# Projection weights in two parts, the first attention unit's loads ahead of the windowed ones, and the last tile's multiplies on VectorE

## The chip, the cores and the metric

The kernel runs on one core of a Trainium2 chip. The metric is the device time of one execution in microseconds (us). The engines named below are TensorE (PE), VectorE (DVE), ScalarE (ACT), GpSimd (POOL) and SyncE (SP), which here only issues DMAs.

## The reference

One layer of a bidirectional encoder on 2048 tokens of width 1024, in float32:

```python
h = rms_norm(x, ln1_g)
z = h @ w_in         # [q_A 512 | k_A 128 | v_A 128 | c_q 384 | c_kv 256 | k_rope 32]
o_A = window_gqa(...)        # |i-j| <= 128, 8 heads, 2 kv heads, table of biases, sink logit
o_B = latent_attention(...)  # q from c_q @ w_qb, k and v from c_kv @ w_kvb, one rotary key
                             # for all heads, 8 heads, dense over 2048 keys
x = x + concat(rms_norm(o_A), rms_norm(o_B)) @ w_o
x = x + expert_choice_ffn(rms_norm(x))   # 16 experts, each takes 256 tokens
```

Queries and keys are RMS-normalised per head; the rotary parts are turned by position.

## The kernel before, in words

The program has three regions. **Region 1** takes the sixteen 128-token tiles one by one: RMSNorm, transposes, the projection with w_in, and from its result everything that attention needs. The result is stored to HBM in transposed form: `kT`, `qT`, `kR` and `v2` for latent attention (stage s3, lines L808 to L830, and stage s2, L720 to L806), `qA`, `kA`, `vA_d` for windowed attention (stage sa, L680 to L718). **Region 2** computes the windowed attention of 16 query tiles (`bounded(t)`, L998 to L1047) interleaved with 32 units of latent attention (8 heads by 4 chunks of 512 queries, `head(h, qc)`, L1107 to L1174). A window tile is two or three pairs of score matmuls (L1016), a table add on DVE (L1021), an exponential on ACT (L1024), adds into `acw` on POOL (L1026, L1028), value matmuls (L1033) and the row sums (L1055, which take `ones` from an operand that depends on the sink row `es`, L1065 and L1066). A latent unit is four groups of rotary matmuls (L1126), score matmuls (L1135), exponentials (L1140), value matmuls (L1150) and adds into `acc` on DVE (L1143, L1145). **Region 3** is w_o, the router and the experts.

Every matmul operand is split into a high part (ACT, L419) and a low part (DVE, L421), and a projection is three products. The w_in weights, split in this way, fill one SBUF tile `WB` of 128 x 23040 words. When the projections of the last tile have run, the same tile is carved anew (class `Views`, L298 to L313) into the bias table, the windowed keys, queries and values, the first unit's queries `qq0`, and the latent keys and values. What is loaded there waits for a marker operation `MK` behind the last projection matmul. For the last tile the transposed results also lie in `WB`; for the others they lie in the two buffers of `th`.

The order of the work on each engine is made by a list planner before the program is built (`Plan.schedule`, L147 to L241). An operation has a cost, a priority (its stage's number plus an offset per stage and engine, `OFF1` for region 1, `OFF2` for region 2) and a list of what it needs; the planner lets each engine take the ready operation of least priority. So a changed cost, need or offset can reorder instructions in the whole region. SP is an engine like the others: a DMA whose data isn't there holds back the DMAs behind it in its queue. In the kernel, SP's DMAs also go round eight completion semaphores, so that each waits until the one eight places ahead has landed.

`PRE_K` is the number of key tiles of the first latent unit that are loaded before the branch that ends region 1 (L1727); the rest of its keys is loaded behind the branch.

Of the kernel before, what the change touches and what calls it, by code (L numbers as in the profile page):

```python
# [21 lines left out]
P = 128  # L22
# [22 lines left out]
PRE_K, PRE_PR = 8, 155  # L45
OFF1 = {'s1S': -41.3, 's2V': 236.2, 's2P': -164.3, 's3V': -16.5, 'saS': 38.9, 's3S': 457.6, 'saV': -26.6, 's3P': -240.0, 'saG': -311.4, 's2G': -35.2, 's1P': -67.4, 's1A': -127.1, 's2A': 17.7, 's2S': -117.5, 's3A': -334.6, 'saA': 265.7, 's1V': -588.0, 'saP': 172.4}
OFF2 = {'bfP': -89.2, 'aG': -6.5, 'awV': -1.5, 'bfS': -57.7, 'bfV': 89.2, 'asP': -33.4, 'awP': -84.8, 'bfA': -1.0, 'bfG': -6.1, 'bvP': 29.3, 'awS': -37.9, 'avP': 28.4, 'afS': 47.0, 'blS': -30.5, 'bV': 10.7, 'pfS': 58.5}
# [211 lines left out]
def build(tc, nc, a, out, dbg=None, upto=9, path="both"):  # L259
# [38 lines left out]
    class Views:  # L298


        def __init__(self):
            carve = carver()
            self.tab = f(carve(8, 384))
            kk = carve(4 * 6 * P)
            self.KK = {n: kk[:, :4 * n * P].rearrange("p (c s) -> p c s", c=4) for n in (4, 6)}
            self.qq0 = carve(3, 512)
            self.va = f(carve(4, 2, 64))
            self.qs = [carve(8, P), None]
            self.kr = carve(4, P)
            v0, k0 = f(carve(NT, VD)), carve(2, SEQ)  # L310
            self.free = WB[:, carve.used[0]:]
            v1, k1 = f(carve(NT, VD)), carve(2, SEQ)
            self.vts, self.kk = [v0, v1], [k0, k1]  # L313
# [36 lines left out]
        def fetch_qq(self, h, qc, qq):  # L350
            src = qT[:, h * HD:h * HD + HD, qc * 512:qc * 512 + 512]

            def go():
# [5 lines left out]
                for j in range(4):  # L359
                    sync.dma_start(q[RD * j:RD * j + RD, 2], src[1, NO:HD])  # L360
# [27 lines left out]
    class Ops(Plan):  # L388
# [25 lines left out]
        def load(self, nbytes, fn, r, w, need=(), pr=None):  # L414
            return self.op("S", 0.5, fn, r, w, need, pr, nbytes)
# [24 lines left out]
    def region1():  # L440
        with ExitStack() as st:
# [16 lines left out]
            WH, WL = (pl.fixed(carve(ND, CW + AW)) for _ in range(2))  # L458
# [39 lines left out]
            load_w(WH, WL, a["w_in"][0][:, AW:], lambda: g1, ND, CW, -30)  # L498
# [4 lines left out]
            load_w(WH, WL, a["w_in"][0][:, :AW], lambda: g1, ND, AW, -8, CW)  # L503
# [23 lines left out]
            MK = pl.fixed(None)  # L527
# [85 lines left out]
            def stage1(t):  # L613
# [26 lines left out]
                def project(c0, n, need):  # L640
                    z = [u_(), u_()]
                    for k in range(ND):
                        xh, xl = xT[k // 4]

                        def mms(k=k, xh=xh, xl=xl):
                            for lh, rh, first, last in ((xh, WH, k == 0, False), (xh, WL, False, False),
                                                        (xl, WH, False, k == ND - 1)):
                                for i in range(2):
                                    pe.matmul(z[i]()[:, :n], lh()[:, k % 4, :], rh()[:, k, c0 + i * n:c0 + (i + 1) * n],  # L649
                                              start=first, stop=last)  # L650

                        pl.mm(6 * n / 2400, mms, [xh, xl, (WH, (k, c0)), (WL, (k, c0))], z, need=need)
# [3 lines left out]
                z = project(0, 336, [zc])  # L656
# [16 lines left out]
            def th_(t, shape, i):  # L673
# [4 lines left out]
                return pl.fixed(V2.free[:shape[0], 1024 * i:1024 * i + 2 * n * P].rearrange("p (a b c) -> p a b c", a=2, b=n))  # L678

            def stage_a(t):  # L680
                s1, project = S[t][3:]
                rows = slice(t * P, (t + 1) * P)
                za = z3([P, 12, 64])
                z = project(CW, 384, [za])
                if t == NT - 1:
                    pl.op("P", 0.0, lambda: None, [], [WH, WL, MK], pr=-99)
# [6 lines left out]
                pl.G(640, lambda: pool.tensor_mul(sq(), za()[:, :10], za()[:, :10]), [(za, 0), (za, 1)], [sq])  # L693
# [10 lines left out]
                pl.G(512, lambda: pool.tensor_mul(za()[:, :8], za()[:, :8], bh(r1()[:, :8], 64)), [r1, (za, 0), (za, 1)],  # L704
                     [(za, 3)])
                for dst, h0, n in ((kA, 8, 1), (qA, 0, 4)):
# [7 lines left out]
                    pl.mm(n * TR, trs, [(za, 2 if h0 else 3)] + ([MK] if t == NT - 1 else []), [tr], need=[th])  # L714
# [5 lines left out]
            def stage2(t):  # L720
                zc, v3, r3 = S[t][:3]
# [86 lines left out]
            def stage3(t):  # L808
# [4 lines left out]
                for i, (src, dst, c0, n) in enumerate(((ks, kT, 0, 4), (qf, qT, 0, 4), (qf, qT, 4, 2))):  # L813
# [7 lines left out]
                    pl.mm(n * TR, trs, [src] + ([MK] if t == NT - 1 else []), [tr], need=[th])  # L821
# [941 lines left out]
```

## Time and profile before

| | |
|---|---|
| time, median of 3 runs | 2586.59 us (2585.72 to 2591.03) |
| profiled execution | 2585.55 us |
| its span (first to last instruction) | 2583.8 us |
| PE busy | 2461.3 us, 95% of the span |
| DVE, ACT, POOL busy | 63%, 46%, 13% |
| region 1 | until about 439.5 us, projections until 428.6 us |
| region 2 | from about 440 us to 1180 us |

A row of a timeline gives an instruction's start, its duration, the engine, the line, the output and the inputs. In square brackets stands how long the engine had been idle before it, and what ended the idle time. SPq rows are the issues of DMAs; the transfer itself ends later. The granted clock is the speed that TensorE was given, 1.00 standing for 2.4 GHz and 0.50 for 1.2 GHz.

### The profile page before, as it was taken

Reading aid. Unit: us, or ns where it says so; the run is one execution under the profiler, and the core shown is the slowest. Engines: PE = TensorE matmul, PEld = TensorE weight load, DVE = VectorE, ACT = ScalarE, POOL = GpSimd, SP = SyncE. Lnnn points to the kernel's source line nnn. Section 1 sums busy time; section 2 is a strip of 40 time slices with the busy share of each in tenths; the row PEclk is TensorE's granted clock in tenths of the full one; section 3 lists DMA queues with packets and bytes.
Section 4 is the critical chain, followed back from the end, with each engine's and each line's share of the span. In section 5 each row is a group of like instructions: output and inputs, shape, how many; then the busy total and the mean of one; then the engine's idle time right before and its main releaser. Section 6 shows DMA issues by size and latency. Waiting matters only on the chain.

```text
span 2583.8 us, 38603 instructions
## 1 busy us (share of the span) xinstructions
PE 2461.3 (95%) x14922; PEld 1962.1 (76%) x14922; DVE 1636.5 (63%) x3024; ACT 1195.1 (46%) x1729; POOL 335.6 (13%) x268
## 2 busy tenths in 40 slices
PE   6999997899999999998997599999999999999998
PEld 5999996344444444446786599999999999999997
DVE  6666665586777767668767765555555555555553
ACT  5444543444444444444444344454554445454442
POOL 2233232121111210000000000000000000000000
PEclk9999998899999999999999699999999999999999
DMA  6433435942442333116543266666666666766662
GB/s 195 131 117 115 120 98 157 212 113 67 104 107 74 90 87 81 55 44 217 174 162 132 74 203 211 204 206 217 215 215 202 223 215 210 226 200 219 220 189 81
DMA packets 348544, 399.40 MB, mean 155 GB/s; under 512 B 43152, under 2 KB 291856, under 8 KB 348224
## 3 DMA queue, kind: packets, MB, share of 16 engines
q1 hardware_dynamic: 339136, 363.03, 44.9%
q0 software_dynamic: 9216, 33.82, 5.4%
q8 instruction: 119, 1.95, 0.3%
q14 instruction: 73, 0.60, 0.1%
HBM read 317.47 MB, written 81.41 MB: 154 GB/s over the span
## 4 chain that ended last, share of the span: by engine, by line
PE 87%; DVE 5%; issue 3%; DMA 2%; ACT 1%; POOL 1%; SPq 1%; POOLq 0%; DVEq 0%; ACTq 0%
PE y L1675 14%; PE u L649 10%; PE gu L1645 9%; PE gu L1646 9%; PE gu L1647 9%; PE sb L1135 9%; PE pv L1150 7%; PE y L1370 6%; PE u L743 3%; PE sb L1126 2%; PE sb L1055 1%; PE tr L1621 1%; PE sb L1016 1%; DVE acc L1145 1%; PE pv L1033 1%
## 5 line engine op out<-in xcount | busy, mean ns | idle before, releaser
L421 DVE TENSOR_TENSOR wlo<-raw,whi 128x2048 fp32r<-128x2048 f32 x192 | 440.0, 2292 | 364.4 <-ACT whi L419 364.4
L1645 PE MATMUL gu<-xh,whi 128*128 128x256 f32 x2048 | 580.9, 284 | 0.0
L1646 PE MATMUL gu<-xl,whi 128*128 128x256 f32 x2048 | 575.1, 281 | 0.0
L1647 PE MATMUL gu<-xh,wlo 128*128 128x256 f32 x2048 | 574.8, 281 | 0.0
L419 ACT ACTIVATE whi<-raw 128x2048 fp32r<-128x2048 f32 x192 | 368.2, 1917 | 276.9 <-PE gu L1646 150.9
L1140 ACT ACTIVATE pp<-sb 128x1024 f32<-128x1024 f32 x256 | 252.6, 1025 | 303.6 <-PE sb L1135 262.3
L1645 PEld LDWEIGHTS gu<-xh,whi 128*128 128x128 f32 x2048 | 385.9, 188 | 0.6
L1646 PEld LDWEIGHTS gu<-xl,whi 128*128 128x128 f32 x2048 | 385.8, 188 | 0.7
L1647 PEld LDWEIGHTS gu<-xh,wlo 128*128 128x128 f32 x2048 | 385.8, 188 | 0.0
L1145 DVE TENSOR_TENSOR acc<-acc,pp 128x1024 f32<-128x1024 f32 x192 | 248.9, 1297 | 125.0 <-ACT pp L1140 115.2
L1675 PE MATMUL y<-whi,aa 128*128 128x512 f32 x1024 | 278.5, 391 | 0.0
L1150 PE MATMUL pv<-pp,WB 128*64 128x512 f32 x1024 | 252.5, 606 | 0.0
L1675 PEld LDWEIGHTS y<-whi,aa 128*128 128x128 f32 x1024 | 191.3, 188 | 40.4
L649 PE MATMUL u<-WB,xh 128*128 128x384 f32 (+1 forms) x1024 | 219.9, 336 | 2.2 <-ACT WB L419 1.4
L649 PEld LDWEIGHTS u<-WB,xh 128*128 128x128 f32 x1024 | 172.3, 190 | 3.4 <-ACT WB L419 1.8
L1370 PE MATMUL y<-whi,aa 128*128 128x512 f32 x512 | 149.0, 403 | 10.9 <-ACT aa L419 8.7
L1675 PE MATMUL y<-wlo,aa 128*128 128x512 f32 x512 | 158.6, 391 | 0.0
L1150 PEld LDWEIGHTS pv<-pp,WB 128*64 128x64 f32 x1024 | 64.1, 136 | 122.6 <-issue 92.3
L1686 POOL DMA_INDIRECT out_dram<-ot,idx x32 | 51.0, 1594 | 792.8 <-ACT ot L1683 702.0
L1135 PE MATMUL sb<-WB 128*128 128x512 f32 x512 | 142.2, 417 | 0.0
L1135 PE MATMUL sb<-qq,WB 128*128 128x512 f32 x512 | 140.0, 416 | 0.0
L649 PE MATMUL u<-WB,xl 128*128 128x336 f32 (+1 forms) x512 | 126.9, 329 | 0.0
(274 smaller groups left out, 3442.8 us busy)
## 6 DMA issues: line engine op xcount, KB each, us to landing
raw<-w_gate SPq DMA_DIRECT2D x64, 1024.0 KB, 5.1
raw<-w_up SPq DMA_DIRECT2D x64, 1024.0 KB, 5.3
raw<-w_down SPq DMA_DIRECT2D x64, 1024.0 KB, 5.1
xt<-x SPq DMA_DIRECT2D x32, 512.0 KB, 4.1
WB<-kT SPq DMA_DIRECT2D x48, 256.0 KB, 4.6
oT_d<-fo SPq DMA_DIRECT2D x64, 128.0 KB, 2.4
ot<-oT_d SPq DMA_DIRECT2D x16, 512.0 KB, 4.2
out_dram<-xt SPq DMA_DIRECT2D x16, 512.0 KB, 2.7
```

The costliest lines, as they stand in the source:

```text
L419: self.A(n, lambda: act.activation(hi(), src(), AF.Copy, scale=sc()), r + list(rs), [w_hi], need, pr, sb)
L421: self.V(n, lambda: dve.tensor_sub(lo(), src(), f(hi())), r + [w_hi], [w_lo], need, pr)
L649: pe.matmul(z[i]()[:, :n], lh()[:, k % 4, :], rh()[:, k, c0 + i * n:c0 + (i + 1) * n], start=first, stop=last)
L1135: pe.matmul(s()[:, j], kk.t[:, c, ksl], qq()[:, c], start=False, stop=c == 1)
L1140: pl.A(1024, lambda s=s, p=p: act.activation(p(), s(), AF.Exp), [s], [p])
L1145: pl.V(1024, lambda p=p: dve.tensor_add(acc(), acc(), p()), [p], [acc])
L1150: pe.matmul(pv()[64 * j:64 * j + 64], vt()[:, 2 * n + j], p()[:, j], start=n == 0, stop=n == 7)
L1370: pe.matmul(pw[i](), o4(l)[:, ks], r_()[:, c:c + 512], start=first, stop=last_)
L1645: pe.matmul(o, c3(hi, ND)[:, k, fs], xh()[:, k], start=k == 0, stop=False)
L1646: pe.matmul(o, c3(hi, ND)[:, k, fs], xl()[:, k], start=False, stop=False)
L1647: pe.matmul(o, c3(lo, ND)[:, k, fs], xh()[:, k], start=False, stop=k == ND - 1)
L1675: pe.matmul(y[i][j](), l()[:, ts], r_()[:, o:o + 512], start=first, stop=last_)
```

## The change

**Weights in two parts.** The weights of w_in are kept as `W1` (the columns of c_q, c_kv and k_rope, the first 10752 words of a row of `WB`) and `WA` (the columns of the windowed heads). `Views` puts `qq0`, the latent keys and values `k0` and `v0`, the rotary key `kr` and the windowed values `va` over `W1`, and the table, windowed keys and queries over `WA`. Two markers take the place of one: `MK1` behind the last matmul with `W1`, `MK2` behind the last with `WA`.

**Loads and priorities.** The first latent unit's loads need `MK1` and the stores of the key tiles they read; they have priority 140 to 142. Twelve key tiles are loaded instead of eight. The windowed keys and queries and the table need `MK2` and have priority 900 and 901, which lies behind the stores of the last tiles. A unit's queries are fetched by five DMAs instead of eight (the last four become one that reads its source four times).

**Last tile.** The multiplies of 640 and 512 columns in stage sa run on DVE for tile 15.

**Region 2.** The windowed tiles' priorities are moved (`step` 26 in place of 27, and `LATE` 14), and an operation without an instruction on an engine "D" of the planner stands for the table's arrival, 8 us into the region's plan. The offsets are other numbers: in `OFF1` s2P goes from -164.3 to -242.7, s3V from -16.5 to 12.0, saV from -26.6 to -2.9; in `OFF2` bfS, awP, bfA, bvP change, and pfV and bA are added.

```diff
-PRE_K, PRE_PR = 8, 155
+PRE_K, PRE_PR = 12, 140
...
+            self.qq0 = carve(3, 512)
+            v0, k0 = f(carve(NT, VD)), carve(2, SEQ)
+            self.kr = carve(4, P)
+            free1 = carve(2560)
+            self.va = f(carve(4, 2, 64))
+            carve(2 * ND * CW - carve.used[0])
             self.tab = f(carve(8, 384))
...
-                for j in range(4):
-                    sync.dma_start(q[RD * j:RD * j + RD, 2], src[1, NO:HD])
+                sync.dma_start(q[:, 2], src[1, NO:HD][None].to_broadcast([4, RD, 512]))
...
-            WH, WL = (pl.fixed(carve(ND, CW + AW)) for _ in range(2))
+            W1 = [pl.fixed(carve(ND, CW)) for _ in range(2)]
+            WA = [pl.fixed(carve(ND, AW)) for _ in range(2)]
...
-                z = project(0, 336, [zc])
+                z = project(W1, 336, [zc])
+                if t == NT - 1:
+                    pl.op("P", 0.0, lambda: None, [], W1 + [MK1], pr=-99)
...
             def stage_a(t):
+                G_, en = (pl.V, dve) if t == NT - 1 else (pl.G, pool)
...
-                    pl.op("P", 0.0, lambda: None, [], [WH, WL, MK], pr=-99)
+                    pl.op("P", 0.0, lambda: None, [], WA + [MK2], pr=-99)
...
-                pl.G(640, lambda: pool.tensor_mul(sq(), za()[:, :10], za()[:, :10]), [(za, 0), (za, 1)], [sq])
+                G_(640, lambda: en.tensor_mul(sq(), za()[:, :10], za()[:, :10]), [(za, 0), (za, 1)], [sq])
...
-            pl.load(1600000, load_tab, [GD, MK], [], pr=PRE_PR + 1)
+            first = sum((KT[t] for t in range(4)), [MK1])
+            most = sum((KT[t] for t in range(PRE_K)), [MK1])
+            K0 = pl.fixed(None)
+            pl.load(P * 6144, V2.fetch_qq(0, 0, lambda: V2.qq0), first, [(K0, 0)], pr=PRE_PR, n=5)
+            pl.load(P * 512 * PRE_K // 4, V2.fetch_kr(0, PRE_K // 4), most, [(K0, 1)], pr=PRE_PR, n=4)
+            pl.load(P * 8 * PRE_K * P, V2.fetch_k(0, 0, PRE_K * P), most, [(K0, 2)], pr=PRE_PR + 1, n=4)
+            pl.load(PRE_K * P * 256, V2.fetch_v(0, 0, PRE_K), most, [(K0, 3)], pr=PRE_PR + 2)
...
+                pl.load(P * 512, V2.fetch_va(t), QA[t] + [MK1], [], pr=PRE_PR + 2)
...
+                    pl.load(64 * 2048, fn, QA[t] + [MK2], [], pr=900)
+            for fn in V2.fetch_q(0):
+                pl.load(64 * 4096, fn, QA[0] + [MK2], [], pr=900)
+            pl.load(1600000, load_tab, [GD, MK2], [], pr=901)
...
+                pl.op("D", 8.0, lambda: None, [], [TAB], pr=-1000, nbytes=1)
...
-            step = 27 if mix else 10
+            step, LATE = (26, 14) if mix else (10, 0)
...
-                base = step * (t + 1)
+                base = step * (t + 1) + LATE
```

SP before, from the last stores of tile 14's windowed heads to the first DMA behind the branch (L322 and L317 load windowed keys and queries, L872 the table, L355 to L364 the first latent unit; `th` and `WB` on the right of an arrow are stores):

```order
L717 DMA kA<-th_5275 128x2x128
L322 DMA WB<-kA 64x4x128 x2
...
L872 DMA WB<-g_d 128x8x384
L317 DMA WB<-qA 64x8x128 x2
L355 DMA WB<-qT 96x512
...
L335 DMA WB<-kT 64x1024
...
L364 DMA WB<-v_63 128x8x64
L717 DMA qA<-th_5352 128x8x128
L824 DMA kT<-WB 128x4x128 x2
L700 DMA vA_d<-va_5416 128x128
...
L717 DMA qA<-WB 128x8x128
L1727 COMPARE_AND_BRANCH
```

The table and the loads stand ahead of the stores of the last tile. SP after the change, from the same kind of store on (L357 to L365 load the first latent unit, L324 and L319 windowed keys and queries, L885 the table):

```order
L725 DMA kA<-th_4983 128x2x128
L357 DMA WB<-qT 96x512
...
L337 DMA WB<-kT 64x1536
...
L365 DMA WB<-v_63 128x12x64
...
L725 DMA qA<-th_5095 128x8x128
L833 DMA kT<-th_5081 128x4x128 x2
...
L324 DMA WB<-kA 64x4x128 x2
...
L725 DMA kA<-th_5399 128x2x128
...
L885 DMA WB<-g_d 128x8x384
L725 DMA qA<-th_5418 128x8x128
...
L1742 COMPARE_AND_BRANCH
...
L337 DMA WB<-kT 64x512
```

The first unit's loads now stand ahead of the remaining stores of tiles 13 and 14, the windowed loads between the stores, and the table ahead of the last three stores, where `qA<-th_5418` is that of tile 14's queries.

PE before at the branch, from the last transposes of region 1 on (L1016 window scores, L1126 rotary, L1135 latent scores, L1033 and L1150 values):

```order
L712 MATMUL tr_5430<-cm,z_1_5126 128x128
L712 MATMUL tr_5433<-cm,z_1_5126 128x128 x4
L1726 TENSOR_LOAD flag_t
L1727 COMPARE_AND_BRANCH
L1016 MATMUL sb_5496<-WB 128x512 x4
L1016 MATMUL sb_5507<-WB 128x512 x4
L1126 MATMUL sb_5537<-WB 128x512 x2
...
L1135 MATMUL sb_5537<-WB 128x512 x4
...
L1033 MATMUL pv_5498<-pp_5497,WB 64x512 x2
L1150 MATMUL pv_5541<-pp_5539,WB 64x512 x2
```

PE after the change at the same place (L1141 rotary, L1150 latent scores, L1031 window scores, L1165 and L1048 values):

```order
L720 MATMUL tr_5417<-cm,z_0_4820 128x128 x4
L720 MATMUL tr_5425<-cm,z_4_5155 128x128 x4
L720 MATMUL tr_5436<-cm,z_4_5155 128x128
L1741 TENSOR_LOAD flag_t
L1742 COMPARE_AND_BRANCH
L1141 MATMUL sb_5493<-WB 128x512 x2
...
L1150 MATMUL sb_5493<-WB 128x512 x4
...
L1031 MATMUL sb_5515<-WB 128x512 x4
...
L1165 MATMUL pv_5497<-pp_5495,WB 64x512 x2
...
L1048 MATMUL pv_5517<-pp_5516,WB 64x512 x2
```

The latent unit's rotary and score matmuls have gone ahead of the window scores, and of the last transposes those of tile 15's windowed heads (`z_4_5155`) now come last.

POOL before, from the last tile's key multiply to the branch (`z_1_5126` is the last tile's windowed projection, `k_2` its latent keys):

```order
L788 TENSOR_TENSOR k_2_5284<-k_2_5284,r_1_5309 128x512
L693 TENSOR_TENSOR z_0_5346<-z_1_5126 128x640
L789 TENSOR_TENSOR k_2_5284<-k_2_5284,gkn 128x512
L791 TENSOR_TENSOR z_4_5237<-z_4_5237,r_1_5309 128x8x32
L792 TENSOR_TENSOR z_2_5340<-z_4_5237,rope_108 128x8x32
L795 TENSOR_TENSOR rt_5395<-z_4_5237,rope_109 128x8x16 x2
L797 TENSOR_TENSOR z_2_5340<-z_2_5340,rt_5395 128x8x32
L704 TENSOR_TENSOR z_1_5126<-z_1_5126,r_1_5379 128x512
L1726 TENSOR_LOAD flag_t
```

POOL after the change, the same stretch:

```order
L797 TENSOR_TENSOR k_2_5267<-k_2_5267,r_1_5293 128x512
L800 TENSOR_TENSOR z_2_5231<-z_2_5231,r_1_5293 128x8x32
L798 TENSOR_TENSOR k_2_5267<-k_2_5267,gkn 128x512
L801 TENSOR_TENSOR z_3_5324<-z_2_5231,rope_108 128x8x32
L804 TENSOR_TENSOR rt_5362<-z_2_5231,rope_109 128x8x16 x2
L806 TENSOR_TENSOR z_3_5324<-z_3_5324,rt_5362 128x8x32
L1741 TENSOR_LOAD flag_t
```

The rows L693 and L704 of the last tile are gone from POOL, and its latent rows follow one another.

## Rows read from the trace of the kernel before

**Rows 1.** The profile's page: the span; busy PE in the 40 slices of 64.6 us; the granted TensorE clock in the same slices; the shares of the chain that ended last.

```profile
span 2583.8 us, 38603 instructions
...
PE   6999997899999999998997599999999999999998
...
PEclk9999998899999999999999699999999999999999
...
PE 87%; DVE 5%; issue 3%; DMA 2%; ACT 1%; POOL 1%; SPq 1%; POOLq 0%; DVEq 0%; ACTq 0%
```

**Rows 2.** Busy time of each engine in stretches of 20 us (in brackets the number of instructions), then the granted clock, the DMA share and GB/s.

```profile
400.00:420.00 20.00, 20.00 (x130) 19.82 (x129) 8.97 (x33) 6.64 (x19) 6.83 (x8) 1.00 0.33 99
420.00:440.00 20.00, 12.78 (x67) 10.62 (x65) 14.95 (x49) 8.56 (x23) 9.00 (x10) 0.81 0.68 191
440.00:460.00 20.00, 9.00 (x20) 5.76 (x20) 3.16 (x3) 3.10 (x4) 2.36 (x1) 0.59 0.94 247
460.00:480.00 20.00, 16.46 (x68) 7.33 (x68) 11.15 (x11) 5.57 (x7) 0.00 (x0) 0.91 0.98 214
480.00:500.00 20.00, 16.68 (x74) 7.63 (x72) 11.90 (x12) 10.02 (x12) 2.35 (x1) 1.00 1.02 222
920.00:940.00 20.00, 16.59 (x67) 6.77 (x65) 13.89 (x12) 7.39 (x8) 4.75 (x2) 0.94 0.49 121
```

**Rows 3.** The same view with stretches of 4 us before the end of the projections, and two long stretches behind them.

```profile
405.00:409.00 4.00, 4.00 (x26) 3.98 (x26) 0.69 (x1) 0.60 (x1) 0.93 (x2) 1.00 0.51 155
417.00:421.00 4.00, 4.00 (x23) 3.79 (x22) 3.82 (x25) 1.35 (x5) 0.00 (x0) 1.00 0.22 66
421.00:425.00 4.00, 4.00 (x25) 3.56 (x24) 3.41 (x11) 3.40 (x12) 1.04 (x1) 1.00 0.09 25
425.00:457.00 32.00, 13.79 (x53) 10.01 (x52) 13.79 (x35) 6.24 (x13) 8.21 (x10) 0.67 0.94 253
433.00:498.00 65.00, 45.19 (x171) 22.75 (x171) 30.63 (x39) 18.86 (x25) 7.70 (x7) 0.79 0.99 229
```

**Rows 4.** Timeline of the end of region 1: start, duration, engine, line, output from inputs, count, and in square brackets how long the engine had been idle and what ended it. The first two rows are the last whole pass of projection matmuls; L693, L704 and L712 belong to the last tile's windowed projection, L787 is a VectorE multiply of the same width as L704.

```profile
427.42 0.86 PE L649 MATMUL u<-WB,xh 128*128 128x384 f32 x4
...
427.79 0.69 DVE L787 TENSOR_TENSOR z<-z,r 128x512 f32<-128x512 f32 x1
...
428.11 0.51 PE L649 MATMUL u<-WB,xl 128*128 128x384 f32 x2
...
428.46 0.60 PE L712 MATMUL tr<-cm,z 128*128 128x128 f32 x4
...
429.44 1.25 POOL L693 TENSOR_TENSOR z<-z 128x640 f32<-128x640 f32 x1
...
436.05 1.15 POOL L704 TENSOR_TENSOR z<-z,r 128x512 f32<-128x512 f32 x1 [1.13 <-DVE r L411]
...
438.00 1.50 PE L712 MATMUL tr<-cm,z 128*128 128x128 f32 x5 [1.48 <-DVE WB L421]
```

**Rows 5.** Issues on SP in the timeline (start and time that the row took on SP), first loads, then stores, then the sink row and w_o behind the branch; and below them two rows of the view of the transfers between 400 and 500 us (count, KB each, median us from issue to landing).

```profile
427.06 1.79 SPq L322 DMA_DIRECT2D WB<-kA  x2
...
431.47 0.43 SPq L872 DMA_DIRECT2D WB<-g_d  x1
...
433.31 2.32 SPq L355 DMA_DIRECT2D WB<-qT  x1
...
447.65 0.43 SPq L364 DMA_DIRECT2D WB<-v  x1
448.20 0.56 SPq L717 DMA_DIRECT2D qA<-th  x1
...
451.59 0.48 SPq L700 DMA_DIRECT2D vA_d<-va  x1
...
468.32 0.36 SPq L1065 DMA_DIRECT2D es<-a_sink  x1
...
WB<-g_d SPq DMA_DIRECT2D x1, 1536.0 KB, 7.6
...
WB<-qA SPq DMA_DIRECT2D x4, 256.0 KB, 8.4
```

**Rows 6.** Timeline of the beginning of region 2: the instructions of PE and ACT that waited longest between 440 and 501 us.

```profile
450.33 1.01 PE L1126 MATMUL sb<-WB 32*128 32x512 f32 x2 [4.74 <-DMA WB<-kR]
...
454.68 1.94 ACT L1024 ACTIVATE pp<-sb 128x1024 f32<-128x1024 f32 x2 [14.54 <-DMA vA_d<-va]
...
462.75 0.50 PE L1126 MATMUL sb<-WB 32*128 32x512 f32 x4
...
472.29 1.08 PE L1055 MATMUL sb<-acw,ones 128*64 128x512 f32 x4 [3.54 <-issue]
...
497.99 1.15 ACT L419 ACTIVATE whi<-raw,gab 128x1024 fp32r<-128x1024 f32 x1 [2.56 <-DMA raw<-w_o]
...
500.09 1.39 PE L1033 MATMUL pv<-pp,WB 128*64 128x512 f32 x4 [3.41 <-ACT pp L1024]
```

**Rows 7.** The view of the waits of PE between 428 and 1180 us (total, times, longest), and one of them in the timeline.

```profile
PE sb L1055 <- POOL acw L1028: 6.8, 7, 2.1
...
PE sb L1055 <- DVE am L1161: 3.2, 1, 3.2
...
554.13 1.08 PE L1055 MATMUL sb<-acw,ones 128*64 128x512 f32 x4 [2.06 <-POOL acw L1028]
```

More of the change, by code (lines that the diff above doesn't have):

```diff
@@ L677, in th_ @@
                 n = shape[2]
-                return pl.fixed(V2.free[:shape[0], 1024 * i:1024 * i + 2 * n * P].rearrange("p (a b c) -> p a b c", a=2, b=n))
+                m = V2.free[i > 1]
+                i = i % 2 if i < 4 else 2
+                return pl.fixed(m[:shape[0], 1024 * i:1024 * i + 2 * n * P].rearrange("p (a b c) -> p a b c", a=2, b=n))
             def stage_a(t):
+                G_, en = (pl.V, dve) if t == NT - 1 else (pl.G, pool)
                 s1, project = S[t][3:]
@@ L720, in stage2 @@
             def stage2(t):
+                G_, en = (pl.V, dve) if t == NT - 1 else (pl.G, pool)
                 zc, v3, r3 = S[t][:3]
@@ L824, in stage3 @@
                     pl.load(n * P * 1024, lambda th=th, dst=dst, c0=c0, n=n: [sync.dma_start(
-                        dst[c, c0 * P:(c0 + n) * P, rows].rearrange("(j p) s -> p j s", p=P), f(th())[:, c]) for c in range(2)], [th], note(KT[t]))
+                        dst[c, c0 * P:(c0 + n) * P, rows].rearrange("(j p) s -> p j s", p=P), f(th())[:, c]) for c in range(2)], [th], note(KT[t]), n=2)
                 tr = tr_()
@@ L1078, in windowed @@
                     if t < NT:
-                        pl.prio, pl.stage = step * (t - 0.8), "af"
+                        pl.prio, pl.stage = step * (t - 0.8) + LATE, "af"
                         fetch(t)
@@ L1099, in latent @@
                     if h == 0:
-                        pl.load(P * 512, V2.fetch_kr(PRE_K // 4, 4), [], [(KR, m) for m in range(PRE_K // 4, 4)])
+                        pl.load(P * 512, V2.fetch_kr(PRE_K // 4, 4), [], [(KR, m) for m in range(PRE_K // 4, 4)], n=4)
                     for c0, c1 in zip(cuts, cuts[1:]):
-                        pl.load(P * 1024 * (c1 - c0), V2.fetch_k(h, c0 * P, c1 * P), [], [(kk, kt) for kt in range(c0, c1)])
+                        pl.load(P * 1024 * (c1 - c0), V2.fetch_k(h, c0 * P, c1 * P), [], [(kk, kt) for kt in range(c0, c1)], n=4 if h < 2 else 3)
                         pl.load((c1 - c0) << 15, V2.fetch_v(h, c0, c1), [], [(vt, kt) for kt in range(c0, c1)])
@@ L1113, in head @@
                 else:
-                    pl.load(P * 6144, V2.fetch_qq(h, qc, qq), [], [qq])
+                    pl.load(P * 6144, V2.fetch_qq(h, qc, qq), [], [qq], n=5)
                 pv = pv_()
```

47 lines of the change are left out of this document (19 added, 28 removed).

## The prediction

> **What bounds the kernel now.** I read the page first: PE is the engine that bounds nearly everything (87% of the chain), and its slices fall below 9 tenths in a few places only: the start, the two slices with a 7 and an 8 that begin at 6 x 64.6 = 388 us and hold the junction of regions 1 and 2, and some around the beginning of region 3, which the change leaves alone [rows 1]. The stretches of 20 us then show what the junction looks like: PE is full until 420, has 12.78, 9.00, 16.46 and 16.68 busy us of 20 in the next four, and a clock of 0.59 in the emptiest. Beside it the DMA share goes from 0.33 to 0.68 and then stays between 0.94 and 1.02 for 60 us [rows 2]. So of the 80 us from 420 to 500, PE idles 25.1, and more is lost because what runs there runs slowly. Just ahead of it the DMAs are nearly empty, 66 and 25 GB/s between 417 and 425 [rows 3]. Last I followed the waits through the timeline. The projections end at 428.6. The last transposes end at 438.00 + 1.50 = 439.5, after two POOL multiplies on the last tile's chain [rows 4]. The first exponential runs at 454.68 after ACT idled 14.54 us, waiting for a store that SP issued only at 451.59, behind all loads [rows 5, 6]. The window's row sums wait for the sink row, issued at 468.32, until 472.29, and the value matmuls of 500.09 wait for ACT, which waited for w_o [rows 6]. The junction is bound by one queue of DMAs that is full from 425 to 498, while stores and loads that are wanted early stand late in it.
>
> **The first unit's loads go ahead.** In bytes by their shapes they are 0.79 MB of queries, 0.20 of the rotary key, 1.57 of keys, 0.39 of values and 0.13 of windowed values: 3.08 MB. Their marker is the last matmul with W1. In the new order 66 matmuls of 384 columns, 18 more of 384, 12 of 512 and 18 transposes stand between it and the end of the projections. Four of 384 start 0.69 us apart from the next two, so one costs 0.17, one of 512 by its columns 0.23, and a transpose 0.60/4 = 0.15 [rows 4]. That is 14.3 + 2.8 + 2.7 = 19.8, so the marker falls at 428.6 - 19.8 = 408.8. From there on DMA is at 0.5 falling to 0.09 [rows 3]; at the 253 GB/s of the full stretch 3.08 MB take 12.2 us, so they land by about 422. They cost PE nothing; its cover is the projections, which run on. Out of the full stretch they take 3.08 MB / 229 GB/s = 13.4 us [rows 3].
>
> **Stores first.** What replaces the wait for a store behind the loads? By the new program's buffers the first exponential reuses memory whose last reader is tile 14's query store, and this now stands behind the table's load, which itself has 3.2 MB of windowed loads and stores ahead of it from 428.5 on (1.0 MB of loads, which before were held at SP's head from 427.06 [rows 5], the rest stores). So the gate is 3.2 + 1.57 + 0.52 = 5.3 MB, at 253 GB/s 20.9 us: 449.4. The bounds: the early end is the store's own price, issued by 438 with the 3.1 us from the store of 451.59 until ACT ran [rows 5, 6], 441; the late end is the old 454.68. Trace rows say that a DMA behind the table shares its time: the windowed queries behind it took 8.4 us for 256 KB, against 7.6 of the table's 1.5 MB [rows 5]. I take 449, so the gate comes 5.7 us earlier.
>
> The Trainium skill, "DMA: Bandwidth & Descriptors", section "Queues, rings and completion order", has a rule that speaks against this order: a ring's descriptors are consumed in order and the completing write lands only after every earlier write of that engine. By that rule the store cannot complete ahead of the table's bytes; without it the gate would open near 441. The 8.4 us agree with the rule; that it does not hold here is the first rival below.
>
> **The last tile on VectorE.** POOL's 1.25 and 1.15 us [rows 4] go. On DVE, 512 columns took 0.69, so 640 take 0.86: the chain is 0.85 shorter, and POOL's latent rows no longer queue behind the 640, 1.25 earlier. But DVE also splits the transposes, which now interleave with the chain in its queue; one split of 512 (0.69, as L787's) in front of it gives most of that back. Bounds: 2.1 us earlier, 0.7 later. I take 1 us, 438.5 in place of 439.5. It is hidden behind the gate of 449, so it counts nothing in the sum.
>
> **Region 2's first 70 us.** PE begins with rotary and latent scores, whose operands have landed, and window scores as soon as keys and queries have; by 449 both are done, cold. In the kernel before, the second group's rotary came 8.1 us after the first exponential and the sums 17.6 after it [rows 6]. The first distance shrinks, since the first unit's scores (3.6 us when cold) now run ahead of it: second group at about 455, 8 earlier. Five query DMAs in place of eight and 3 MB less bring the sink row's issue to about 456, so its stall goes, and the sums follow the matmuls, at 461.5 by counting them at their warm rates: 10.8 earlier. At 497.99 it is w_o that sets the pace, and that waits for bytes only: 13.4 us less of them, of which I keep 12.4, since issue distances remain. So PE's 500.09 becomes 487.7. Behind it the work is the same, so -12.4 is the junction's term. Its bounds: 5.7, if only the gate's gain carries, and 18, if the idle 25.1 [rows 2] shrink to the wait of 449 - 442.
>
> **The rest of region 2.** The planner's new costs change the interleaving. One wait of 3.2 us for `am`, with a clock of 0.94 around it [rows 2, 7], is tied to an order that the new program doesn't have; it goes, and with it about as much again in slow matmuls: -6.8. The order in which it comes to wait for POOL's `acw` (four window scores' values, then the sums at once, 2.06 us at 554.13) stands in the new program three times instead of twice: +2.1 and a slower clock behind it, +3.9 to +5 altogether. I take +4.4. Together -2.4, with 4 us either way, as such waits come and go by the order (7 of them gave 6.8 us [rows 7]). Region 1 up to 408 and region 3 have the same rows and cost the same.
>
> **Sum.** 2585.55 is the profiled execution's own time, 1.75 above its span, and 1.04 below the median of the three runs. -12.4 - 2.4 = -14.8: 2570.8 on its scale, 2571.8 on the median's. I predict 2572.
>
> **Rivals.**
> - *Bytes don't set the gate.* If the store may pass the table, the first exponential runs at 441 to 443, PE waits for almost nothing, and the junction gives 18 instead of 12.4: 2566. For it: the store is only 0.52 MB, and PE would be ready; against it: the 8.4 us of the loads behind the table [rows 5].
> - *The queue's end keeps its pace.* If w_o's load comes from SP's order (each DMA waits for the one eight ahead, and for buffers that region 2's own work frees) and not from bytes, only the gate's 5.7 us carry: -5.7 - 2.4 gives 2578.5. For it: ACT's wait for w_o is the last of the chain here [rows 6]. Against it: DMA is at 1.02 in that stretch [rows 2].
> - *The change moves the queue and nothing else.* The gate's store is late again, at 454, because the table goes later, and the saved wait and the added ones in the rest cancel: 2584 to 2587.
> - *Slower: region 2's new order.* Its place is the sums behind a tile's last window pair, where PE waits for two adds on POOL (2.1 us at 554.13 [rows 7]) and then runs at a lower clock, 3.9 us each in all. The gain of 14.8 is used up by four more such places, and 2591.8 is passed from six more than counted. With six more, 6 x 3.9 = 23.4 - 14.8: 2595. For it: 14 tiles have such a place, and `step`, the offsets and `LATE` all moved. Against it: the order shows three of the pattern, and DVE and POOL idle much.
> - *Also later: stores behind the new loads.* Sixteen DMAs stand ahead of tile 13's and 14's stores, whose buffers ACT needs for tile 14's last transposes at 426. At 0.88 us each (SP's seventeen from 433.31 to 448.20 [rows 5]) the stores go at 422.9, and land with the 3.1 us of above at 426, just in time; where the loads go slower by a fifth, ACT is some 3 us late, and the junction with it. That takes 12.4 to 9, within the range.
>
> **Numbers.** My forecast has 0.50, with its own range of 2567 to 2577; the gate that opens early 0.17, the queue that keeps its pace 0.16, the moved queue 0.10, the slower order 0.07. What a measurement of this kernel can tell from no change is 0.2%, 5.2 us: faster means below 2581.4. The first three cases give faster nearly whole (0.82), the fourth and the edges of the third give 0.11 for the same, and 0.07 is slower. From 2562, a good deal below the first rival, to 2583, the range leaves out some 0.15 at the top and little below.
>
> **What would show it.** In the changed profile: the first unit's query load issued near 409 and its values landed by 423; DMA above 0.9 between 410 and 422, with PE still full; the first latent scores before 445; the first exponential at 449 behind a store; no wait for the sink row; the w_o split near 485; PE from 500 on as in the rows before, only earlier. It would be wrong if PE lost time before 428, if the first exponential came after 453, or if PE's later waits for `acw` came to more than 15 us.

## The result, and the profile after

The changed kernel took 2571.39 us (median of 4 runs, 2568.39 to 2574.19) against 2586.15 for the kernel before: a ratio of 0.9943, with an interval of 0.9931 to 0.9955. Two more jobs, on two chips, gave 0.9937 (0.9923 to 0.9950) and 0.9956 (0.9943 to 0.9970). Predicted were 2572, between 2562 and 2583. The profiled execution took 2574.19 us, the slowest of the four; its span is 11.4 us shorter than that of before.

The page of the changed kernel: the span, busy PE and the granted clock in 40 slices of 64.3 us. Slices 7 and 8 of PE have 8 and 8 tenths for 7 and 8 [rows 1]; elsewhere PE and its clock differ by a tenth at most, in the first slice and early in region 3.

```profile
span 2572.4 us, 38488 instructions
...
PE   7999998899999999998997699999999999999998
...
PEclk8999998899999999999998799999999999999999
```

The stretches of 20 us that answer to [rows 2], then four that answer to [rows 3] (PE, PEld, DVE, ACT, POOL busy, clock, DMA share, GB/s):

```profile
400.00:420.00 20.00, 20.00 (x125) 19.45 (x125) 13.05 (x51) 8.40 (x24) 6.83 (x8) 1.00 0.81 177
420.00:440.00 20.00, 13.97 (x76) 11.81 (x74) 14.12 (x45) 7.54 (x20) 7.23 (x8) 0.79 0.82 235
440.00:460.00 20.00, 16.36 (x52) 8.31 (x48) 4.88 (x5) 4.91 (x5) 2.35 (x1) 0.70 0.81 232
460.00:480.00 20.00, 18.39 (x84) 9.02 (x84) 14.73 (x15) 9.51 (x11) 0.00 (x0) 1.00 1.15 193
480.00:500.00 20.00, 12.88 (x46) 5.18 (x42) 9.37 (x8) 6.17 (x6) 4.82 (x2) 0.74 0.80 211
409.00:413.00 4.00, 4.00 (x29) 3.97 (x27) 2.05 (x8) 3.49 (x11) 1.30 (x3) 1.00 0.95 225
421.00:425.00 4.00, 4.00 (x24) 4.00 (x24) 3.54 (x15) 1.75 (x6) 0.38 (x1) 1.00 0.85 267
425.00:457.00 32.00, 22.34 (x82) 13.89 (x82) 13.21 (x29) 9.02 (x16) 8.48 (x8) 0.68 0.80 232
433.00:498.00 65.00, 48.84 (x182) 24.02 (x183) 32.98 (x40) 21.91 (x28) 7.16 (x3) 0.79 0.93 220
```

DMA now has 0.81 and not 0.33 in 400 to 420, and 0.85 at 267 GB/s where it moved 25 GB/s; PE stays full beside it. 440 to 460 holds 16.36 busy us of PE in place of 9.00. But 480 to 500 holds 12.88 in place of 16.68, at a clock of 0.74. Of the five stretches it is the one in which PE does less than before.

The timeline of the changed kernel: the first load of the first unit, the last matmuls with `W1`, the first store behind the unit's loads, the last transposes, the table's load and the store of tile 14's queries behind it, the first rotary matmul, the first exponential, the sink row's load, the second group's rotary, the first row sums, w_o's loads, its first split on ACT, and the third window values of tile 1 (they answer to [rows 4 to 6]).

```profile
402.56 0.33 SPq L357 DMA_DIRECT2D WB<-qT  x1
...
408.55 0.47 PE L652 MATMUL u<-WB,xl 128*128 128x336 f32 x2
...
414.22 3.07 SPq L725 DMA_DIRECT2D qA<-th  x1
...
436.59 1.30 PE L720 MATMUL tr<-cm,z 128*128 128x128 f32 x5 [1.14 <-ACT th L420]
...
438.74 0.44 SPq L885 DMA_DIRECT2D WB<-g_d  x1
439.27 0.60 SPq L725 DMA_DIRECT2D qA<-th  x1
...
439.62 0.80 PE L1141 MATMUL sb<-WB 32*128 32x512 f32 x4 [1.73 <-DMA qT<-WB]
...
448.13 1.94 ACT L1155 ACTIVATE pp<-sb 128x1024 f32<-128x1024 f32 x2 [9.65 <-DMA qA<-th]
...
455.57 0.46 SPq L1080 DMA_DIRECT2D es<-a_sink  x1
...
455.97 0.19 PEld L1141 LDWEIGHTS sb<-WB 32*128 32x128 f32 x4 [1.05 <-issue]
...
463.55 1.08 PE L1070 MATMUL sb<-acw,ones 128*64 128x512 f32 x4 [1.61 <-issue]
...
482.47 1.09 SPq L1280 DMA_DIRECT2D raw<-w_o  x2
...
491.39 1.15 ACT L420 ACTIVATE whi<-raw,gab 128x1024 fp32r<-128x1024 f32 x1 [6.27 <-DMA raw<-w_o]
...
493.50 0.30 PEld L1048 LDWEIGHTS pv<-pp,WB 128*64 128x64 f32 x4 [8.00 <-ACT pp L1039]
```

The first unit's loads went out from 402.56, and by the trace PE waited for none of them when it first used them, at 439.62, but 1.73 us for a store. The first exponential ran at 448.13 for 454.68, the second group at 455.97 for 462.75, the sums at 463.55 for 472.29. Then ACT stood from 485.12 until w_o had landed, 491.39, and PE, in the same order of work as at 500.09 of before, went on at 493.50: only 6.6 us earlier. In the kernel before, w_o was issued at 492.44, and among SP's waits between 405 and 505 us is one for PE's score matmuls:

```profile
492.44 1.09 SPq L1265 DMA_DIRECT2D raw<-w_o  x2
...
SPq L317 <- PE sb L1135: 3.7, 2, 3.1
```

PE's waits in the changed kernel from 428 to 1180 that answer to [rows 7]:

```profile
PE sb L1070 <- POOL acw L1043: 8.9, 8, 2.2
PE pv L1048 <- ACT pp L1039: 8.3, 2, 7.1
```

The wait for `am` of 3.2 us is gone, that for `acw` went from 6.8 to 8.9. The last row sums of region 2 begin at 1158.7, before at 1170.1: 11.4 earlier, the whole gain of this execution; region 3 adds nothing.

### The profile page after: what moved, and what is told of

Read it like the earlier page. It is cut to its first block, busy times and chain, and to the rows that moved or that the text cites. A ratio compares the mean times of both kernels' runs of the same rounds, so it can differ in the third digit from the quotient of the medians.

```text
span 2572.4 us, 38488 instructions
## 1 busy us (share of the span) xinstructions
PE 2460.0 (96%) x14922; PEld 1961.5 (76%) x14922; DVE 1637.0 (64%) x3026; ACT 1195.9 (46%) x1729; POOL 334.5 (13%) x266
## 4 chain that ended last, share of the span: by engine, by line
PE 72%; DVE 4%; issue 3%; DMA 1%; POOL 1%; ACT 1%; SPq 0%; POOLq 0%; DVEq 0%; ACTq 0%
PE y L1690 14%; PE gu L1660 9%; PE gu L1661 9%; PE gu L1662 9%; PE sb L1150 9%; PE pv L1165 8%; PE y L1385 6%; PE sb L1141 2%; PE sb L1070 1%; PE tr L1636 1%; PE sb L1031 1%; PE pv L1048 1%; POOL acw L1043 1%; DVE sb L1036 1%; DVE acc L1160 1%
## 5 line engine op out<-in xcount | busy, mean ns | idle before, releaser
L1165 PE MATMUL pv<-pp,WB 128*64 128x512 f32 x1024 | 253.2, 608 | 0.0
L652 PE MATMUL u<-WB,xh 128*128 128x336 f32 (+1 forms) x1024 | 221.9, 339 | 2.0 <-ACT WB L420 1.4
L1165 PEld LDWEIGHTS pv<-pp,WB 128*64 128x64 f32 x1024 | 63.8, 136 | 122.1 <-issue 91.8
L1150 PE MATMUL sb<-WB 128*128 128x512 f32 x512 | 140.8, 413 | 0.0
L1150 PE MATMUL sb<-qq,WB 128*128 128x512 f32 x512 | 137.9, 411 | 0.0
```

The costliest lines, as they stand in the source:

```text
L652: pe.matmul(z[i]()[:, :n], lh()[:, k % 4, :], rh()[:, k, i * n:(i + 1) * n], start=first, stop=last)
L1150: pe.matmul(s()[:, j], kk.t[:, c, ksl], qq()[:, c], start=False, stop=c == 1)
L1165: pe.matmul(pv()[64 * j:64 * j + 64], vt()[:, 2 * n + j], p()[:, j], start=n == 0, stop=n == 7)
```

## The experiments

The theory at this point: the junction's gain is the 3.08 MB moved out of the full stretch of DMA, with most of the stores ahead of the table; region 2's order adds a little; and the wait for w_o takes part of it back. The rivals: region 2's order carries the gain; or the tail on VectorE does; or the store, not the bytes, was all. Each kernel below is the changed one with the edit shown, unless it says otherwise; each was run against the kernel before on the same chip.

**The changed kernel again.** 

> The changed kernel itself, timed again beside the edits below. If the wait for w_o is the program's and no accident, PE waits again some 7 us ahead of the last window values of tile 1, with w_o landing near 491 us, and the ratio to the kernel before is again 0.993 to 0.9955. If that wait was an accident of one execution, PE's wait there is under 4 us.

Measured: 2568.54 us (2567.83 to 2572.37), ratio 0.9937 (0.9923 to 0.9950). The first exponential, w_o's split and the window values in it:

```profile
447.00 1.94 ACT L1155 ACTIVATE pp<-sb 128x1024 f32<-128x1024 f32 x2 [10.04 <-DMA qA<-th]
...
487.01 1.15 ACT L420 ACTIVATE whi<-raw,gab 128x1024 fp32r<-128x1024 f32 x1 [3.51 <-DMA raw<-w_o]
...
489.12 0.29 PEld L1048 LDWEIGHTS pv<-pp,WB 128*64 128x64 f32 x4 [5.24 <-ACT pp L1039]
```

The wait is there again, but 4.4 us and not 7.1: w_o landed 5.3 us after its issue at 481.69, where it took 8.9 in the first profile. So neither of the two forms of the expectation held; the wait belongs to the program, its length varies with the run (a third profile has 5.2 us). The window values came 11.0 us earlier than before's 500.09.

**The w_o split later.**

```diff
+        HELD = pl.fixed(None)
+        pl.op("D", 10.0, lambda: None, [RAW], [HELD], pr=-1000, nbytes=1)
...
-            pl.split(1024, lambda sl=sl: HI()[:, sl], lambda sl=sl: LO()[:, sl], lambda sl=sl: RAW()[:, sl], [RAW, SM],
+            pl.split(1024, lambda sl=sl: HI()[:, sl], lambda sl=sl: LO()[:, sl], lambda sl=sl: RAW()[:, sl], [RAW, SM, HELD],
```

> The two halves of the first w_o split are planned 10 us later, so that on ACT they stand behind the tile's last window exponential and on DVE behind five adds. Theory (w_o's landing took back about half of the junction's gain, through ACT's order): PE's wait of 7.1 us at 486.4 goes, and the slow clock behind it (0.74 in 480 to 500), so the time falls by 6 to 9 us against the changed kernel, to 2562 to 2565. Rival (PE is short of operands there anyway, keys, queries or the table add): the wait moves to another releaser and the time falls by under 2 us.

Measured: 2570.44 us (2565.34 to 2572.32), ratio 0.9941 (0.9928 to 0.9955). The profiled run, which was the fastest, shows tile 1's last two exponentials together and its window values without a break:

```profile
482.60 2.15 ACT L1039 ACTIVATE pp<-sb 128x1024 f32<-128x1024 f32 x2 [1.63 <-DVE sb L1036]
...
482.99 2.89 PE L1048 MATMUL pv<-pp,WB 128*64 128x512 f32 x12
```

The wait is gone at its place: the twelve value matmuls end at 482.99 + 2.89 = 485.9, where the changed kernel began the last four at 493.50. (The 10 us of the expectation is not what holds the split: in the planner an operation with bytes is done 2.2 us after the planned transfers are through, whatever its cost. The split moved behind the exponentials all the same.) The median doesn't show it: three of the five runs had a granted clock of 0.977 over the span and took 2570 to 2572, two had 0.980 and took 2565 and 2567. The local part of the theory is shown, its 6 to 9 us in the time are not.

**The small loads in region 1.** The loads of the two gains, ln2's gain and the router's weights follow tile 6's store of v; the planner's order is unchanged.

```diff
-        pl.load(600000, small, [], [SM])
+        pl.load(600000, lambda: None, [], [SM])
...
+                pl.load(P * 2048, lambda: (sync.dma_start(v2[rows], vv()), small0() if t == 6 else None), [vv], note(KT[t]))
...
```

> The four small loads (two gains, ln2's gain, the router's weights) are issued in region 1 behind tile 6's store of v instead of just ahead of w_o. Theory (their many small packets hold the rings: DMA share 0.71 at 69 GB/s from 480 to 484): w_o lands about 3 us earlier than 491.4, PE's wait before it shrinks from 7.1 to about 4, and the time falls by 3 us, to 2568. Rival (w_o waits for the bytes ahead of it only): it lands within 1 us of before and the time stays.

Measured: 2568.88 us (2564.61 to 2573.72), ratio 0.9933 (0.9919 to 0.9946). DMA from 480 to 484 in the changed kernel's first profile and in this one:

```profile
480.00:484.00 4.00, 4.00 (x18) 1.91 (x16) 3.70 (x5) 1.03 (x1) 0.00 (x0) 1.00 0.71 69
480.00:484.00 4.00, 4.00 (x19) 1.93 (x17) 2.57 (x3) 2.07 (x3) 0.00 (x0) 1.00 0.94 237
```

w_o's loads, w_o's split and the window values in this one:

```profile
479.96 3.19 SPq L1280 DMA_DIRECT2D raw<-w_o  x2
...
488.03 1.15 ACT L420 ACTIVATE whi<-raw,gab 128x1024 fp32r<-128x1024 f32 x1 [0.46 <-DMA raw<-w_o]
...
490.14 1.08 PE L1054 MATMUL pv<-pp,WB 128*64 128x512 f32 x4 [1.32 <-ACT pp L1045]
```

The four small loads are most of the 0.71 share with 69 GB/s: engines busy, and nearly no bytes (3083 of the 3421 packets in this stretch of the first profile are under 512 B). Without them w_o is issued 2.5 us earlier than in the first profile and 1.7 earlier than in the second, lands at 488.0, and PE waits 1.3 us. But from the issue to the split it still takes 8.1 us, where it took 8.9 and 5.3 with the small loads ahead of it, and the window values come 1.0 us later than in the second profile. So an earlier issue is shown, a faster landing is not. PE's shorter wait is in part its own later arrival (the second window scores waited 6.2 us for ACT, 3.6 in the first profile), and the time isn't told apart from the changed kernel.

**The table behind the stores.**

```diff
-            pl.load(1600000, load_tab, [GD, MK2], [], pr=901)
+            pl.load(1600000, load_tab, [GD, MK2] + QA[14] + QA[15], [], pr=901)
```

> The bias table's load goes behind the last three stores of region 1 instead of ahead of them; nothing else moves. Theory (the first exponential opens when the store behind the table completes, and that store shares the table's time): the first exponential opens at about 443 instead of 448.1, the window's table add goes from 446.6 to 449 to 450, and the time changes by -3 to +1 us. Rival (the store was late for another reason, the bytes of all that was issued before): the first exponential stays at 447 to 449.

Measured: 2571.55 us (2569.92 to 2572.86), ratio 0.9945 (0.9932 to 0.9959). The store of tile 14's queries, the first exponential, the first table add and the first window values:

```profile
436.89 0.40 SPq L725 DMA_DIRECT2D qA<-th  x1
...
440.75 1.02 ACT L1155 ACTIVATE pp<-sb 128x1024 f32<-128x1024 f32 x1 [4.17 <-DMA qA<-th]
...
449.88 1.23 DVE L1036 TENSOR_TENSOR sb<-sb,WB 128x1024 f32<-128x1024 f32 x1 [12.54 <-DMA WB<-g_d]
...
452.22 1.97 PE L1048 MATMUL pv<-pp,WB 128*64 128x512 f32 x4 [5.88 <-ACT pp L1039]
```

The gate opens at 440.75, even earlier than the 443 expected, so it was the table ahead of the store. Of the 7.4 us, 2.4 are the store's earlier issue, 436.89 for 439.27, as this execution came earlier to its stores; from the issue to the exponential it took 3.9 us and not 8.9, so the table ahead of it cost about 5. By the rule of the Trainium skill, "DMA: Bandwidth & Descriptors", section "Queues, rings and completion order", a store's completing write lands only after the earlier writes of its engines; the step from 8.9 us to 3.9 agrees with it. The gain is nil all the same: the table add goes from 446.61 to 449.88, and the window values, which stand next in PE's order, wait 5.9 us.

**All weights freed at once.** The first unit's loads and those of the windowed values need both markers.

```diff
-            first = sum((KT[t] for t in range(4)), [MK1])
-            most = sum((KT[t] for t in range(PRE_K)), [MK1])
+            first = sum((KT[t] for t in range(4)), [MK1, MK2])
+            most = sum((KT[t] for t in range(PRE_K)), [MK1, MK2])
...
-                pl.load(P * 512, V2.fetch_va(t), QA[t] + [MK1], [], pr=PRE_PR + 2)
+                pl.load(P * 512, V2.fetch_va(t), QA[t] + [MK1, MK2], [], pr=PRE_PR + 2)
```

> The first latent unit's loads and the windowed values wait for the end of all projection matmuls again (both markers), as if the weights were in one part; the rest is the changed kernel. Theory (the gain is 3.08 MB taken out of the full stretch): DMA falls back to under 0.5 from 410 to 425, the table and the first window add come about 12 us later than 446, and the time goes back by 9 to 14 us, to 2578 to 2583. Rival (the gain is the order of the stores and of region 2, the early loads only fill an empty stretch): the time stays within 4 us of the changed kernel, under 2574.

Measured: 2582.37 us (2579.25 to 2583.57, 11 runs), ratio 0.9985 (0.9976 to 0.9994). DMA from 410 to 425 and the stretch from 433 to 498, then the first exponential, the first window scores and the first table add:

```profile
410.00:425.00 15.00, 15.00 (x90) 14.16 (x89) 12.98 (x52) 8.03 (x24) 2.30 (x2) 1.00 0.49 147
433.00:498.00 65.00, 41.14 (x151) 20.48 (x150) 25.49 (x32) 17.41 (x22) 2.37 (x1) 0.75 0.95 199
```

```profile
448.95 1.94 ACT L1155 ACTIVATE pp<-sb 128x1024 f32<-128x1024 f32 x2 [10.61 <-DMA qT<-WB]
...
458.61 3.68 PE L1031 MATMUL sb<-WB 128*128 128x512 f32 x8 [10.21 <-DMA WB<-qA]
...
464.82 1.23 DVE L1036 TENSOR_TENSOR sb<-sb,WB 128x1024 f32<-128x1024 f32 x1 [25.73 <-DMA WB<-g_d]
```

11 of the 15 us are gone again. The table is issued at 454.52 for 438.74, its add comes 18 us later than in the changed kernel, and PE has 41.14 busy us between 433 and 498 for 48.84. SP's stores of tiles 13 and 14 go ahead of the loads in this kernel, so it is not those stores that cost. The early loads, which only the division of the weights allows, carry most of the gain.

**Region 2's numbers of before.** Old `OFF2`, step 27, `LATE` 0, no stand-in for the table.

```diff
...
-            step, LATE = (26, 14) if mix else (10, 0)
+            step, LATE = (27, 0) if mix else (10, 0)
```

> Region 1 of the changed kernel, region 2 with the old offsets, step 27, no LATE and no stand-in for the table: region 2 begins with the window scores. Theory (the loads carry the junction, region 2's order some 2 us later on): the first exponential is a window's, behind the table at 448 to 449, nothing of the latent unit is done by then on ACT, the junction loses 2 to 4 us and the rest 2.4: 2572 to 2576. Rival (the order carries nothing): within 1.5 us of the changed kernel. Rival (the order carries most): over 2578.

Measured: 2576.38 us (2570.66 to 2577.02), ratio 0.9965 (0.9952 to 0.9979): 5 us more than the 2571 of the changed kernel (the mean of its three medians), and 0.4 us past the expectation's 2576. Four of its five runs took 2576 to 2577, the fifth 2570.66, a time that the changed kernel has too. The profile is of that fastest run, so it doesn't show the whole loss; among PE's waits it shows this one:

```profile
PE sb L1070 <- DVE am L1176: 3.2, 1, 3.2
```

The wait for `am` is back, as the prediction had tied it to that order.

**Region 2's numbers on the kernel before.** The same numbers, put into the kernel before. 

> The kernel before with only region 2's new numbers (offsets, step 26, LATE 14, the stand-in); region 1 and its loads as before. Theory (the order pays only with early loads): the latent unit's rotary at the head of PE waits for the rotary key until 450, the first exponential stays at 454 to 456, the junction gains nothing, the rest between -4 and +2: 2581 to 2588. Rival (the order carries most): under 2578.

Measured: 2588.63 us (2586.90 to 2591.57, 11 runs), ratio 1.0015 (1.0006 to 1.0024). The first rotary matmul and the first exponential:

```profile
449.68 1.41 PE L1128 MATMUL sb<-WB 32*128 32x512 f32 x4 [10.62 <-DMA WB<-kR]
...
453.99 1.94 ACT L1142 ACTIVATE pp<-sb 128x1024 f32<-128x1024 f32 x2 [14.29 <-DMA vA_d<-va]
```

PE waits 10.6 us for the rotary key, which is loaded late there, and the exponential is where it was. So the same order is worth about 5 us with early loads and costs 2.5 without them. The run with both markers, on the same chip, is 6.3 us under this one: that is the worth of the other edits with late loads (the offsets, the five query DMAs, the twelve key tiles, the last tile, the loads behind most stores). Of these only the last tile was undone alone.

**The last tile on POOL.**

```diff
-                G_, en = (pl.V, dve) if t == NT - 1 else (pl.G, pool)
+                G_, en = pl.G, pool
...
```

> The last tile's two multiplies run on POOL again, the rest is the changed kernel. Theory (this edit is hidden behind the gate at 447 to 448): the last transposes end 1 to 2 us later than 437.9, the first exponential moves by under 1.5 us, and the time stays within 1.5 us of the changed kernel. Rival (the tail decides when the stores and the table are issued): the exponential and the time come 2 to 3 us later.

Measured: 2569.58 us (2567.24 to 2571.34), ratio 0.9937 (0.9924 to 0.9951), the same as the changed kernel. The last transposes and the first exponential:

```profile
435.62 1.09 PE L720 MATMUL tr<-cm,z 128*128 128x128 f32 x4 [0.73 <-DVE th L422]
...
446.59 1.94 ACT L1155 ACTIVATE pp<-sb 128x1024 f32<-128x1024 f32 x2 [9.25 <-DMA qA<-th]
```

The edit is worth nothing here. The transposes end at 435.62 + 1.09 = 436.7, in the two profiles of the changed kernel above at 437.9 and 436.4, so the 1 to 2 us that the expectation had for them did not come, and the exponential runs 0.4 us ahead of the earlier of theirs. The planner moved SP's order with the edit (the table is issued at 432.76 and not 438.74, the store of tile 14's queries at 441.29 and not 439.27), so this is the worth of the edit with its order, not of the two multiplies by themselves.

**Both edits of the w_o part.** 

> Both edits of the w_o part at once: the first w_o split planned later, and the four small loads issued in region 1. Theory (w_o's wait in ACT's order took back part of the junction's gain): no wait of PE over 2 us between 480 and 500, the table's and the sink's places as in the changed kernel, the last row sums of the windows at 961 to 964 instead of 966.6 to 969, and 3 to 6 us less than the changed kernel: 2563 to 2567. Rival (what is won there is lost again by slower clock or other waits later in region 2): the row sums' end as in the changed kernel and the time within 2 us of 2570.

Measured: 2565.82 us (2564.74 to 2566.97), ratio 0.9927 (0.9913 to 0.9940), within the expectation; PE's longest wait between 480 and 500 is 0.2 us.

**The second group ahead, and the table last.** Beside the two edits of the run above, the table goes behind the stores, the window scores need the table in the plan, and the stand-in has 1.5 MB:

```diff
-                pl.op("D", 8.0, lambda: None, [], [TAB], pr=-1000, nbytes=1)
+                pl.op("D", 0.1, lambda: None, [], [TAB], pr=-1000, nbytes=1500000)
...
-                    pl.mm(4 * U, score, [qs, (KK, (kt % 4, 0)), (KK, (kt % 4, 1))], [s], need=[p, pv])
+                    pl.mm(4 * U, score, [TAB, qs, (KK, (kt % 4, 0)), (KK, (kt % 4, 1))], [s], need=[p, pv])
```

> The edits of the run beside it, and the table's load behind the last stores, with region 2 planned as if the table came behind 1.5 MB: the second group of the first latent unit goes ahead of the window scores. Theory (with a store ahead of the table the first exponential opens at 441, and only the window's own operations wait for the table): the first exponential at 440 to 442, the second group's rotary at about 446 instead of 454 to 456, 4 to 7 us off the junction, 2557 to 2562. Rival (the new order of the later tiles costs as much in waits for the adds on POOL): the junction gains and the time stays at 2563 to 2570.

Measured: 2577.91 us (2576.61 to 2583.07, 9 runs), ratio 0.9975 (0.9965 to 0.9985). Its first exponential, second group and the first window scores of tile 1:

```profile
440.36 1.94 ACT L1161 ACTIVATE pp<-sb 128x1024 f32<-128x1024 f32 x2 [4.76 <-DMA qA<-th]
...
441.15 0.92 PE L1147 MATMUL sb<-WB 32*128 32x512 f32 x4
...
473.92 3.75 PE L1037 MATMUL sb<-qs,WB 128*128 128x512 f32 x8 [7.28 <-DMA qs<-qA]
```

The opening is as hoped, the second group at 441.15 and not 455.97. Then PE reaches tile 1's window scores before their queries have landed and waits 7.3 us, the wait for `am` is back, and the gain is more than spent. Both the theory and its rival missed: no one had counted the loads that an earlier PE meets too soon.

**Twice on one chip.** The changed kernel: 

> The changed kernel once more, beside the next run on the same chip. Theory (its times fall into two groups by the granted clock): some runs at 0.977 with 2570 to 2574, some at 0.979 to 0.980 with 2566 to 2569, median 2568 to 2572.

The kernel with both edits of the w_o part: 

> The kernel with both edits of the w_o part once more, on the same chip as the changed kernel. Theory (the wait for w_o is gone, and with it the dips of the clock behind it): median 2564 to 2567, all runs at 0.979 or above, 3 to 5 us under the changed kernel. Rival (chance of the first job): within 1.5 us of the changed kernel.

Measured on the same chip: 2573.57 us (2568.64 to 2575.84, ratio 0.9956, 0.9943 to 0.9970) and 2567.01 us (2563.90 to 2567.30, ratio 0.9933, 0.9920 to 0.9947). The stretch from 480 to 500 in the first and in the second:

```profile
480.00:500.00 20.00, 14.84 (x57) 5.80 (x56) 11.36 (x10) 7.25 (x8) 4.82 (x2) 0.83 0.82 209
```

```profile
480.00:500.00 20.00, 19.79 (x86) 8.79 (x85) 14.92 (x13) 10.56 (x11) 4.75 (x2) 1.00 0.82 231
```

PE is busy for 19.79 us at full clock in place of 14.84 at 0.83. All ten runs of the kernel with both edits lie between 2563.90 and 2567.30, all fourteen of the changed kernel between 2567.83 and 2575.84. So it beats both kernels, the changed one by 6.6 us on this chip and the one before by 18 to 19. The intervals of the ratios overlap (0.9913 to 0.9947 over its two jobs, 0.9923 to 0.9970 over the changed kernel's three), so the 6.6 are settled no better than that. Neither edit alone stands apart from the changed kernel in its times, so how much of it each carries is open.

## Why the prediction was right, point by point

- **Loads ahead.** Right. The last matmul with W1 was to end at 408.8; it ended at 408.55 + 0.47 = 409.0. The loads went out even earlier, at 402.56: `qq0` lies over a piece of W1 that had been read for the last time by then, which the prediction hadn't looked at. That they carry most of the gain is shown by the run with both markers (11 of 15 us back).
- **The gate at 449.** Right, 448.13, 447.00 and 448.52 in three profiles, and for the reason given: with the table behind the store it opens at 440.75, about 5 us of that by the table. The rival in which bytes don't set the gate fell with that run, and with it its 2566: a gate that opened early, with the table later, gave nothing.
- **The tail on VectorE at nothing.** Right: nothing, shown by its undoing, which moved SP's order too.
- **Second group 455, sums 461.5.** 455.97 and 463.55. "Its stall goes" was wrong: 1.6 us of the sink row's wait remain.
- **PE at 487.7 in place of 500.09, -12.4.** This term was sized too large. It came at 493.50, 489.12 and 491.71 in three profiles: -6.6, -11.0 and -8.4. The step that failed is "that waits for bytes only". w_o was issued 10.0, 10.8 and 10.3 us earlier, not 12.4. Ahead of it SP's order waits for PE too, as the second rival had said, and PE itself was 8.7, 10.4 and 8.6 us ahead at the sums; that this is all of the difference no run isolates. Then ACT's split came 8.9, 5.3 and 7.5 us after the issue, where the kernel before took 497.99 - 492.44 = 5.6. The small loads are not shown to be what stretched it: they stand ahead of w_o in the kernel before as well, and without them it took 8.1. What did is open. What the run with the split later shows is how the landing reaches PE: through ACT's order, and with another order the wait is gone.
- **The rest of region 2, -2.4 with 4 either way.** To the last row sums it was -4.8, -2.8 and -2.5 (1158.7, 1156.3 and 1159.2 less 1170.1 and less the junction's part). The wait for `am` went, that for `acw` grew by 2.1 as counted. The clock has its part in the first: between 500 and 1160 it has no stretch of 20 us under 1.00, the other two have two each, the kernel before has five. So the sum came out nearer than its terms: in the first profile -6.6 and -4.8, where -12.4 and -2.4 had been said. The three spans are 11.4, 13.2 and 12.0 us shorter than the one of before, and the medians of the three jobs are 2571.4, 2568.5 and 2573.6. That the first of them lies within 1 us of 2572 is luck; that they lie in the range is not.
- **The other rivals.** The moved queue had the gate at 454. PE was full until 428, so no store behind the new loads held it, and the order added 2.1 us of waits for POOL. That region 2's numbers alone can make it slower is shown: 1.0015 on the kernel before. The rule that stood against the change (the store behind the table) held, and its price was in the forecast.
- The front says that the stand-in for the table is due 8 us into the plan. In the planner an operation with bytes is done when its bytes are, so the 8 us only keep "D" busy. With 1.5 MB in place of one byte, and with window scores that need the table in the plan, the order changed: that is the run with the second group ahead.

## What to carry to other kernels

Where one stretch has a full DMA queue and the stretch ahead of it an empty one, ask what keeps the loads from starting: here it was one buffer freed as a whole, and freeing it in parts was worth 11 us, with an order of region 2 that uses the early loads. Then look at what stands ahead of a store or a load that someone waits for, in its own queue: here a transfer of 1.5 MB held a store back by about 5 us, as surely as a missing operand. And an engine that gets ahead meets the next load sooner: count the loads behind the place that you free.

## What was not expected of the hardware

- The DMA share says how busy the engines are, not what they move: 0.71 at 69 GB/s from 480 to 484, and 1.11 at 358 GB/s from 444 to 448, in the same profile.
- The same waits do not always cost clock. The kernel before has waits of 1.17 and 2.06 us at 543.5 and 554.1 and a clock of 0.91 in that stretch [rows 7]; the first profile of the changed kernel has 1.18 and 2.05 us at 538.0 and 548.7, and 1.00 from 520 to 560. Its runs lie apart by as much as 8 us, from 0.976 to 0.980 of the clock over the span. What decides it in one run or the other, no run here shows.
